# A hybrid decoder layer: side lanes load a step ahead, low-half stores one weight later, lane transposes tied to main products

## The chip, the core and the metric

The kernel runs on one core of a Trainium2 chip. The metric is the time of one execution on the device in microseconds (us). The kernel before was run three times: 2049.04, 2053.64 and 2055.61 us, median 2053.64 us. One of its executions was also taken by the hardware profiler; views of it are called the profile or the trace here.

## The reference

The layer works on 2048 tokens of width 1024 in float32. Cut to what is computed:

```python
hn = rms_norm(h, mix_pre_g)
proj = hn @ w_in                      # 1024 -> 512 q, 128 k, 128 v, 2 x 512 conv
attn_out = sliding_window_attention(q, k, v, attn_sinks, rel_bias)   # window 128, 8 heads
conv_out = conformer_conv(u, ...)     # GLU, causal depthwise conv of 31 taps,
                                      # LayerNorm over channels, silu, 512 x 512
mixed = jnp.concatenate([attn_out, conv_out], axis=-1) @ w_out
h = h + rms_norm(mixed, mix_post_g)
hn = rms_norm(h, ffn_pre_g)
ff = (jax.nn.silu(hn @ w_gate) * (hn @ w_up)) @ w_down               # inner width 2816
h = h + rms_norm(ff, ffn_post_g)
```

## The kernel before

Every matrix product keeps float32 accuracy by splitting each operand into a high and a low half and adding three matmuls: high by high, high by low, low by high (`three`, L170; `product`, L846). So a weight that is loaded (tile `raw`, two buffers) is turned into a tile `w` (six buffers) of two halves: ScalarE copies the high half (L110), GpSimd or VectorE subtracts it for the low half (L112 or the helper of L85). The first time that a weight of w_in or w_out is used, the low half is also stored to DRAM (`lo_in`, `lo_out`, L114, issued from SyncE, whose queue is called SP here); later uses load it (L109) instead of subtracting again. `weight` (L120) issues the load of `raw` and calls `split_w` for its two parts.

Tokens are taken in four tiles of 512. The labels behind the @ of a tile's name tell the stage:

- A0 to A3: the product with w_in. B0 to B3: attention. T0 to T3: the 31 taps of the convolution, on VectorE, whose result is stored to `y_scr` (L547).
- C0 to C3 (`stage_tail`): four blocks of `y_scr` are loaded (tile `fc`, three buffers, L559), transposed on TensorE into the one bank `ct` (`turner`, L531), evicted by ScalarE into `yt` (L532), normalised, transposed back (`conv_tail`, L584) and multiplied by the pointwise weights.
- W0 to W3 (`stage_w`): the product with w_out. Its inputs come from `mixT` in DRAM, two of eight blocks at a time (tile `fa` in W0, `at` of two buffers in W1 to W3, L679), and are split into halves by `acts` (L681 and VectorE). Two weights and eight output banks follow for each two blocks; the first banks are evicted into `mid` by ScalarE (L652). The norm at its end uses x@W (L735, GpSimd).
- H0 and H2: the normed rows of two tiles (`hn_scr` in DRAM) become the operands of the feed-forward part, which is computed by seven products of halves of its matrices instead of eight, so that sums of column blocks are needed. `load_cols` (L755) loads one block of 128 columns, `turned` transposes it in four pieces of 128x128 (L777) into a bank `tr`, ScalarE evicts it (L797). `stage_h_plain` makes the operands B11 and B21 and stores them to `hT`; `stage_h_sums` loads them back (`own`, L812) and makes B22 and the sums T1 to T4.
- F (`stage_pre`, `stage_p1`, L846) and G (`stage_p2`, L1116): the products with w_gate and w_up, and with w_down, for tiles 0 and 1, then for tiles 2 and 3.

The order of the work is written as generators. One main generator (`run`) emits A0 to A3, W1, F, G, F, G. Beside it stand lanes (`Lane`): B, the taps, C, W0, W2, W3, H. Each `yield` of the main generator gives its estimated time to every lane as credit, and a lane emits its next step while it has credit; the step's own `yield` takes its cost away again. So the numbers behind `yield` in a lane are its pacing. When all is emitted, a scheduler orders the instructions of each engine by emission order as priority and by when their inputs and buffers are expected to be ready. An ordering dependency without a semaphore (`after_first`, "NoSync") can force one instruction behind another. On the chip, each engine takes its instructions in the built order, and so do the queues that issue DMAs.

The tiles are in rings of few buffers: `raw` 2, `w` 6, `at` 2, `fc` 3, `fa` 4, `chl` 5, `gb` 2; the banks are `mm` 4, `tr` 3, `ct` 1.

Of the kernel before, what the change touches and what calls it, by code (L numbers as in the profile page):

```python
# [12 lines left out]
F32 = mybir.dt.float32  # L13
# [12 lines left out]
P = 128  # L26
# [11 lines left out]
def layer_kernel(ctx, tc, x, xT, cols, rows, sinks, relb, onehot, w_in, w_pw, w_out, w_gate, w_up, w_down, out):  # L38
# [62 lines left out]
    vtt = dve(nc.vector.tensor_tensor)  # L101
    vts = dve(nc.vector.tensor_scalar)
    ptt = nc.gpsimd.tensor_tensor
    mat = nc.tensor.matmul

    def split_w(raw, tag, low=None, made=False, on_pool=True):
        w = tag if not isinstance(tag, str) else hl(tag)
        if made:
            nc.sync.dma_start(w[:, 1].bitcast(F32), low)  # L109
        act(w[:, 0], raw, AF.Copy)  # L110
        if not made:
            (ptt if on_pool else vtt)(w[:, 1], raw, w[:, 0].bitcast(F32), ALU.subtract)  # L112
            if low is not None:
                nc.sync.dma_start(low, w[:, 1].bitcast(F32))  # L114
# [42 lines left out]
    def after_first(first, r):  # L157
        tc.add_manual_dep(
            r.ins,
            first.ins.name,  # L160
            mybir.DependencyInfo(mybir.DependencyClass.NoSync, mybir.DependencyReason.DATA),
            reason="both halves of the array start together",
        )

    def three(o, pairs, first=True, last=True):
# [361 lines left out]
    def turner(yt, ycs):  # L527
        def turn(c):
            b = ct()
            for s in range(4):  # L530
                nc.tensor.transpose(b[:, s * P : (s + 1) * P], ycs[c][:, s * P : (s + 1) * P], ident)  # L531
# [18 lines left out]
    def stage_tail(t):  # L550
        L = f"C{t}"
        lab[0] = L
        yt = t_("yt", (P, 4, 4 * P))
        ycs = []
        turn = turner(yt, ycs)
        for c in range(4):
            lab[0] = L
            y = f2("fc")
            nc.sync.dma_start(y, y_scr[c, :, t * T : (t + 1) * T])  # L559
            ycs.append(y)  # L560
            turn(c)
            yield 0.5
        yield from conv_tail(t, yt)

    def conv_tail(t, yt):
# [15 lines left out]
        for c in range(4):  # L581
            b = ct()
            for s in range(4):
                nc.tensor.transpose(b[:, s * P : (s + 1) * P], yt[:, s, c * P : (c + 1) * P], ident)  # L584
# [85 lines left out]
    def stage_w(w, spill, G, atag, htag, mtag, bank_of, norm=None, ready=None):  # L670
        L = f"W{w}"
        lab[0] = L
        acc = [f4(atag) for _ in range(4)]

        def acts(gi):
            aa = []
            for c in range(G * gi, G * gi + G):
                m = f2(mtag)
                nc.sync.dma_start(m, mixT[c, :, w * T : (w + 1) * T])  # L679
                a = hl(htag)  # L680
                act(a[:, 0], m, AF.Copy)  # L681
                vtt(a[:, 1], m, a[:, 0].bitcast(F32), ALU.subtract)
                aa.append([a])
            return aa

        nxt = acts(0)
        for gi in range(KC // G):
            aa = nxt
            for n in range(2):
                lab[0] = L  # L690
                if n == 1 and gi + 1 < KC // G and not (ready and G * gi + G == 4):
                    nxt = acts(gi + 1)
                ws = weight(w_out[2 * gi : 2 * gi + 2, :, n * T : (n + 1) * T].rearrange("c p t -> p c t"),
                            lo_out[n, 2 * gi : 2 * gi + 2], w > 0)
                yield from block_half(acc, list(zip(aa, ws)), n, gi == 0, L, bank_of)
            if ready and G * gi + G == 4:
                for i, c in enumerate(ready()):
                    if i == Q0 // 2:
                        ld.until("C1")
                        lab[0] = L  # L700
                        nxt = acts(gi + 1)
                    yield c
        tail = norm_w(w, spill, acc, mtag)
        if norm:
            norm(tail)
        else:
            yield from tail
# [62 lines left out]
    }  # L770
    COLTAG = {0: ["fc", "at", "fc", "at"], 2: ["fc", "at", "fc", "at"]}

    def turned(w, k, bank_of, tag):
        c = load_cols(w, k, tag)
        b = bank_of()
        for s in range(4):
            nc.tensor.transpose(b[:, s * P : (s + 1) * P], c[:, s], ident)  # L777
        return b

    def op_tile(ws, ops, n, k, spare):  # L780
# [23 lines left out]
    def stage_h_sums(ws, ops):  # L804
        L = f"H{ws[0]}"
        spare = {}
        for k in range(4):
            lab[0] = L
            ct_ = COLTAG[ws[0]]
# [12 lines left out]
            lab[0] = L  # L822
            stt(r[:, 0], b12, g1, own[0], ALU.mult, ALU.subtract)
# [410 lines left out]
    class Lane:  # L1234
# [12 lines left out]
        def pump(self, dt):  # L1247
# [3 lines left out]
            while self.items and self.credit > 0:  # L1251
# [5 lines left out]
                p0 = tc.cur_priority  # L1257
                tc.cur_priority = p0 + self.lag
                paced[0] = self.lag > 0
                try:  # L1260
                    c = next(gen)
                    self.credit = 0.0 if c is None else self.credit - c
# [2 lines left out]
                    self.items.pop(0)  # L1265
                tc.cur_priority = p0
                paced[0] = False

        def until(self, name):
            while name not in self.done:  # L1270
                assert self.items, name
                n, gen, needs = self.items[0]
                assert not needs or needs(), n
                for c in gen:
                    assert c is not None
                self.done[n] = clk[0]
                self.items.pop(0)

# [182 lines left out]
```

## Time and profile before

| | |
|---|---|
| time, median of three runs | 2053.64 us |
| the profiled execution's own time | 2048.51 us |
| its span | 2046.7 us |
| its mean granted TensorE clock | 0.987 |
| TensorE busy | 1962.1 us, 96% |
| VectorE busy | 1504.6 us, 74% |
| ScalarE busy | 985.5 us, 48% |
| GpSimd busy | 397.9 us, 19% |
| DMA, mean rate | 221 GB/s |

In the profile PE is TensorE's matmuls and transposes, PEld its weight loads, which overlap them, DVE VectorE, ACT ScalarE, POOL GpSimd, and SP the queue of SyncE that issues most of the DMAs. A line such as L777 is a line of the kernel before; L85 is the helper through which every VectorE instruction is recorded, so VectorE's work is told apart by tile names. "x@W<-fa@W,x@W" means that a tile x of a W stage is written from tiles fa and x. In a row of waits, the three numbers are us in all, times, and the longest. The granted clock (PEclk) is the share of TensorE's full clock that its throttle let through.

### The profile page before, as it was taken

What the parts mean: (1) busy time and instruction counts of PE and PEld (TensorE: products, weight loads), DVE (VectorE), ACT (ScalarE), POOL (GpSimd) and SP (SyncE); (2) the same over time, 40 slices, a digit from 0 to 9 for tenths busy, and PEclk for the clock granted to TensorE, in tenths of its full rate; (3) what the DMA queues carried; (4) which work ended last, traced back from release to release, by engine and by line L of the source; (5) the groups of instructions that cost most, each with busy time, mean ns of one, the idle gap of its engine ahead of it and who ended that gap; (6) DMA issues with size and microseconds to landing.
All of it is one profiled execution on the core that took longest, in us unless ns stands there. A gap on an engine that the chain in (4) does not pass through costs nothing. (4 is left out here: it accounts for less than half of the span.)

```text
span 2046.7 us, 27185 instructions
## 1 busy us (share of the span) xinstructions
PE 1962.1 (96%) x8826; PEld 1566.1 (77%) x8826; DVE 1504.6 (74%) x2641; ACT 985.5 (48%) x1938; POOL 397.9 (19%) x442
## 2 busy tenths in 40 slices
PE   8999999999988999999989999989999999999997
PEld 6877766776667778778868778877788888888886
DVE  5999896995885889887649985577666665545558
ACT  5355455456546633333346457456644433345443
POOL 4011223333111300000001012115423323221001
PEclk9999999999999999999999999999999999999999
DMA  8787645678559876884486778688954453266654
GB/s 307 257 297 232 201 135 175 191 241 277 189 156 335 284 236 235 287 273 160 140 262 199 230 256 294 188 284 288 343 185 155 160 164 114 99 233 218 203 188 149
DMA packets 235902, 451.44 MB, mean 221 GB/s; under 512 B 23496, under 2 KB 49264, under 8 KB 235760
## 3 DMA queue, kind: packets, MB, share of 16 engines
q1 hardware_dynamic: 215216, 419.30, 62.5%
q10 hardware_dynamic: 20544, 30.42, 4.0%
q8 instruction: 69, 1.13, 0.2%
q14 instruction: 73, 0.60, 0.1%
HBM read 330.60 MB, written 119.02 MB: 220 GB/s over the span
## 5 line engine op out<-in xcount | busy, mean ns | idle before, releaser
L85 DVE SCALAR_TENSOR_TENSOR fc@C<-glu@C,colt,fc@C 128x512 f32<-128x512 f32 x480 | 370.1, 784 | 3.5
L846 PE MATMUL mm@F<-hl@H,w@F 128*128 128x512 f32 x1056 | 253.3, 390 | 2.5 <-ACT mm@F L886 1.6
L1116 PE MATMUL mm@G<-hl@G,hl@G 128*128 128x512 f32 x924 | 230.7, 399 | 8.1 <-DVE x@G L85 5.2
L846 PEld LDWEIGHTS mm@F<-hl@H,w@F 128*128 128x128 f32 x1056 | 197.6, 188 | 44.8 <-ACT mm@F L886 2.4
L170 PE MATMUL mm@A<-hl@A,w@A 128*128 128x512 f32 x840 | 207.2, 398 | 5.4 <-ACT w@A L110 1.6
L1116 PEld LDWEIGHTS mm@G<-hl@G,hl@G 128*128 128x128 f32 x924 | 175.0, 192 | 47.2 <-ACT hl@G L759 7.3
L1116 PE MATMUL mm@G<-w@G,hl@G 128*128 128x512 f32 x876 | 199.7, 389 | 0.4 <-DVE w@G L85 0.4
L759 ACT ACTIVATE w@F<-chl@F 128x512 fp32r<-128x512 f32 x220 | 134.9, 624 | 134.8 <-PE mm@F L846 125.8
L1116 PEld LDWEIGHTS mm@G<-w@G,hl@G 128*128 128x128 f32 x876 | 164.4, 188 | 34.9 <-DVE w@G L85 0.9
L170 PEld LDWEIGHTS mm@A<-hl@A,w@A 128*128 128x128 f32 x840 | 155.9, 189 | 42.4 <-ACT w@A L110 2.2
L85 DVE TENSOR_TENSOR w@F<-chl@F,w@F 128x512 fp32r<-128x512 f32 x198 | 146.3, 743 | 34.0 <-ACT w@F L759 33.5
L846 PE MATMUL mm@F<-ql@H,w@F 128*128 128x512 f32 x528 | 128.5, 392 | 10.2 <-ACT w@F L759 5.8
L846 PE MATMUL mm@F<-mid@H,w@F 128*128 128x512 f32 x528 | 130.4, 392 | 2.5 <-ACT mm@F L886 1.7
L846 PE MATMUL mm@F<-p@H,w@F 128*128 128x512 f32 x528 | 131.8, 395 | 0.0
L846 PE MATMUL mm@F<-x@H,w@F 128*128 128x512 f32 x528 | 125.8, 391 | 2.3 <-ACT fa@F L908 2.3
L846 PEld LDWEIGHTS mm@F<-ql@H,w@F 128*128 128x128 f32 x528 | 98.7, 188 | 33.5 <-ACT w@F L759 6.7
L846 PEld LDWEIGHTS mm@F<-mid@H,w@F 128*128 128x128 f32 x528 | 98.3, 188 | 25.6 <-ACT mm@F L886 3.8
L846 PEld LDWEIGHTS mm@F<-p@H,w@F 128*128 128x128 f32 x528 | 101.0, 192 | 22.0 <-ACT at@F L1007 0.6
L846 PEld LDWEIGHTS mm@F<-x@H,w@F 128*128 128x128 f32 x528 | 98.7, 188 | 23.6 <-ACT fa@F L908 2.8
L170 PE MATMUL mm@W<-w@W,hl@W 128*128 128x512 f32 x384 | 102.1, 411 | 7.5 <-ACT hl@W L681 7.4
L110 ACT ACTIVATE w@A<-raw@A 128x512 fp32r<-128x512 f32 x110 | 67.7, 627 | 85.3 <-PE mm@A L170 57.6
L170 PE MATMUL tr@W<-w@W,ql@W 128*128 128x512 f32 x384 | 99.4, 398 | 6.2 <-ACT mid@W L652 5.2
(301 smaller groups left out, 3375.8 us busy)
## 6 DMA issues: line engine op xcount, KB each, us to landing
mids<-fa@F SPq DMA_DIRECT2D x154, 256.0 KB, 2.8
raw@A<-w_in SPq DMA_DIRECT2D x55, 512.0 KB, 4.8
w@A<-lo_in SPq DMA_DIRECT2D x84, 256.0 KB, 3.5
fc@G<-mids SPq DMA_DIRECT2D x77, 256.0 KB, 3.5
fa@G<-mids SPq DMA_DIRECT2D x75, 256.0 KB, 4.3
gb@F<-keeps SPq DMA_DIRECT2D x72, 256.0 KB, 4.3
raw@W<-w_out SPq DMA_DIRECT2D x32, 512.0 KB, 5.4
w@W<-lo_out SPq DMA_DIRECT2D x48, 256.0 KB, 4.1
```

The costliest lines, as they stand in the source:

```text
L85: r = op(*args, **kw)
L110: act(w[:, 0], raw, AF.Copy)
L170: mat(o, a, b, start=first and i == 0, stop=last and i == n - 1)
L759: act(w[:, 0], x, AF.Copy)
L846: mat(o, w[:, a, ks], op[k][:, b], start=first and n == 0, stop=n == 11, skip_group_check=not first)
L1116: mat(banks[b], p_, q_, start=start and z == 0, stop=stop and z == 2, skip_group_check=True)
```

## The change

Three things are changed.

1. Ties. `mat` now remembers the last matmul that was not emitted by a lane (`lead_pe`). `tied(r)` puts `r` behind it by an ordering dependency without a semaphore. The first of every four transposes of a lane is tied: in `turner` (L531), `conv_tail` (L584) and `turned` (L777).
2. Stores. The store of a weight's low half (L114) is not emitted with the weight but at the next call of `weight`, ahead of what that call emits, and it is tied to the last main matmul emitted by then.
3. Loads. `stage_tail` loads block c+1 of `y_scr` before it transposes block c; `stage_h_plain` loads two column blocks ahead, `stage_h_sums` one step ahead (`own` and two column blocks); `stage_w` splits `acts` into `loads` and `acts`. In W0, loads and conversion stay at the second weight of a pair; in W1 to W3 the loads go to the first weight, the conversions stay at the second. In W1's middle, where eight pieces of F are put in, the loads stay at piece 4 and the conversions go to piece 6. Pacing changes with it: C's blocks cost 1.5 instead of 0.5 and begin with 2.0, and the H stages begin with 3.0.

```diff
-    mat = nc.tensor.matmul
+    inlane = [False]
+    lead_pe = [None]
+
+    def mat(*args, **kw):
+        r = nc.tensor.matmul(*args, **kw)
+        if not inlane[0]:
+            lead_pe[0] = r
+        return r
+
+    def tied(r):
+        if lead_pe[0] is not None and lead_pe[0] is not r:
+            after_first(lead_pe[0], r)
+        return r
+
+    later = []
+
+    def defer(n, emit):
+        later.append([n, emit])
+
+    def run_later():
+        for item in later:
+            item[0] -= 1
+        while later and later[0][0] <= 0:
+            later.pop(0)[1]()
...
             if low is not None:
-                nc.sync.dma_start(low, w[:, 1].bitcast(F32))
+                defer(1, lambda: tied(nc.sync.dma_start(low, w[:, 1].bitcast(F32))))
         return w
 
     def weight(src, low, made, raw=None, on_pool=True):
+        run_later()
         if raw is None:
...
         def turn(c):
             b = ct()
             for s in range(4):
-                nc.tensor.transpose(b[:, s * P : (s + 1) * P], ycs[c][:, s * P : (s + 1) * P], ident)
+                r = nc.tensor.transpose(b[:, s * P : (s + 1) * P], ycs[c][:, s * P : (s + 1) * P], ident)
+                if s == 0:
+                    tied(r)
...
+        def fetch(c):
+            if c < 4:
+                lab[0] = L
+                ycs.append(f2("fc"))
+                nc.sync.dma_start(ycs[c], y_scr[c, :, t * T : (t + 1) * T])
+
+        fetch(0)
+        yield 2.0
         for c in range(4):
-            lab[0] = L
-            y = f2("fc")
-            nc.sync.dma_start(y, y_scr[c, :, t * T : (t + 1) * T])
-            ycs.append(y)
+            fetch(c + 1)
+            lab[0] = L
             turn(c)
-            yield 0.5
+            yield 1.5
...
-        nxt = acts(0)
+        nxt = acts(loads(0))
         for gi in range(KC // G):
             aa = nxt
+            own = gi + 1 < KC // G and not (ready and G * gi + G == 4)
             for n in range(2):
                 lab[0] = L
-                if n == 1 and gi + 1 < KC // G and not (ready and G * gi + G == 4):
-                    nxt = acts(gi + 1)
+                if n == (w == 0) and own:
+                    ms = loads(gi + 1)
+                if n == 1 and own:
+                    nxt = acts(ms)
...
                     if i == Q0 // 2:
                         ld.until("C1")
-                        lab[0] = L
-                        nxt = acts(gi + 1)
+                        ms = loads(gi + 1)
+                    if i == Q0 - 2:
+                        nxt = acts(ms)
                     yield c
...
+        cols = {}
+
+        def fetch(k):
+            if k < 4:
+                lab[0] = L
+                cols[k] = load_cols(ws[0], k + off, COLTAG[ws[0]][k] if ws[0] else "fa")
+
+        fetch(0)
+        fetch(1)
+        yield 3.0
         for k in range(4):
             lab[0] = L
-            b = turned(ws[0], k + off, tr, COLTAG[ws[0]][k] if ws[0] else "fa")
+            b = turned(cols.pop(k), tr)
+            fetch(k + 2)
...
+        def fetch(k):
+            if k < 4:
+                lab[0] = L
+                own = t_("chl", (P, 2, T))
+                nc.sync.dma_start(own, hT[ws[0] // 2][k :: 4].rearrange("j p t -> p j t"))
+                got[k] = own, load_cols(ws[1], k, COLTAG[ws[0]][0]), load_cols(ws[1], k + 4, COLTAG[ws[0]][1])
+
+        fetch(0)
+        yield 3.0
         for k in range(4):
...
-            own = t_("chl", (P, 2, T))
-            nc.sync.dma_start(own, hT[ws[0] // 2][k :: 4].rearrange("j p t -> p j t"))
+            own, c12, c22 = got.pop(k)
             own = own[:, 0], own[:, 1]
-            b12 = turned(ws[1], k, tr, ct_[2])
-            b22 = turned(ws[1], k + 4, tr, ct_[3])
+            b12 = turned(c12, tr)
+            b22 = turned(c22, tr)
...
             act(b[:, 0], b22, AF.Copy, scale=g2)
+            fetch(k + 1)
             yield 1.5
...
                 paced[0] = self.lag > 0
+                inlane[0] = True
                 try:
                     c = next(gen)
...
                 paced[0] = False
+                inlane[0] = False
```

More of the change, by code (lines that the diff above doesn't have):

```diff
@@ L161, in after_first @@
             mybir.DependencyInfo(mybir.DependencyClass.NoSync, mybir.DependencyReason.DATA),
-            reason="both halves of the array start together",
+            reason="order",
         )
@@ L583, in conv_tail @@
             for s in range(4):
-                nc.tensor.transpose(b[:, s * P : (s + 1) * P], yt[:, s, c * P : (c + 1) * P], ident)
+                r = nc.tensor.transpose(b[:, s * P : (s + 1) * P], yt[:, s, c * P : (c + 1) * P], ident)
+                if s == 0:
+                    tied(r)
             th = f2("fc")
@@ L673, in stage_w, with loads, acts @@
         acc = [f4(atag) for _ in range(4)]
-        def acts(gi):
+        def loads(gi):
+            lab[0] = L
+            ms = []
+            for c in range(G * gi, G * gi + G):
+                ms.append(f2(mtag))
+                nc.sync.dma_start(ms[-1], mixT[c, :, w * T : (w + 1) * T])
+            return ms
+        def acts(ms):
+            lab[0] = L
             aa = []
-            for c in range(G * gi, G * gi + G):
-                m = f2(mtag)
-                nc.sync.dma_start(m, mixT[c, :, w * T : (w + 1) * T])
+            for m in ms:
                 a = hl(htag)
@@ L771, in layer_kernel, with turned @@
     COLTAG = {0: ["fc", "at", "fc", "at"], 2: ["fc", "at", "fc", "at"]}
-    def turned(w, k, bank_of, tag):
-        c = load_cols(w, k, tag)
+    def turned(c, bank_of):
         b = bank_of()
         for s in range(4):
-            nc.tensor.transpose(b[:, s * P : (s + 1) * P], c[:, s], ident)
+            r = nc.tensor.transpose(b[:, s * P : (s + 1) * P], c[:, s], ident)
+            if s == 0:
+                tied(r)
         return b
@@ L806, in stage_h_sums @@
         spare = {}
+        got = {}
+        def fetch(k):
+            if k < 4:
+                lab[0] = L
+                own = t_("chl", (P, 2, T))
[3 more added lines that the diff above has]
+        yield 3.0
         for k in range(4):
             lab[0] = L
[L809 removed]
             g1, g2 = g_ffn[:, k : k + 1], g_ffn[:, k + 4 : k + 5]
[L811 to L812 removed]
+            own, c12, c22 = got.pop(k)
             own = own[:, 0], own[:, 1]
[L814 to L815 removed]
+            b12 = turned(c12, tr)
+            b22 = turned(c22, tr)
             r = t_("chl", (P, 2, T))
@@ L1273, in until @@
                 assert not needs or needs(), n
+                inlane[0] = True
                 for c in gen:
                     assert c is not None
+                inlane[0] = False
                 self.done[n] = clk[0]
```

## The prediction

> **What bounds the kernel now.** I read first the busy times and the slices of the page.
>
> ```profile
> span 2046.7 us, 27185 instructions
> PE 1962.1 (96%) x8826; PEld 1566.1 (77%) x8826; DVE 1504.6 (74%) x2641; ACT 985.5 (48%) x1938; POOL 397.9 (19%) x442
> PE   8999999999988999999989999989999999999997
> ```
>
> TensorE is busy for 96% of the span. Adding up every idle stretch between its records gives 73.5 us, all of it before 1500 us, so the last quarter has nothing to win. An undisturbed stretch (1700 to 1720) holds 90 main products of 128x512 in 20.00 us: 0.222 us each, the price of one matmul below. The change removes no instruction; it can only win from idle time and from what follows it. So I read next TensorE's waits (line that waits, what it waits for: us in all, times, longest).
>
> ```profile
> PE tr@B L494 <- POOL p@B L476: 9.6, 5, 4.5
> PE mm@W L170 <- ACT hl@W L681: 7.4, 3, 4.0
> PE mm@F L846 <- ACT w@F L759: 5.8, 2, 3.2
> PE mm@G L1116 <- DVE x@G L85: 5.2, 1, 5.2
> PE tr@W L170 <- ACT mid@W L652: 5.2, 1, 5.2
> PE ct@C L531 <- DMA fc@C<-y_scr: 3.2, 1, 3.2
> ```
>
> These are single stalls, not a steady loss. The windows around the 5.2 us wait in W2 (PE busy, PEld, DVE, ACT, POOL, then granted clock, DMA share, GB/s) show what a stall costs besides itself:
>
> ```profile
> 1045.00:1050.00 5.00, 5.00 (x25) 3.81 (x23) 3.40 (x6) 1.52 (x3) 0.00 (x0) 1.00 0.83 243
> 1051.00:1056.00 5.00, 0.00 (x0) 0.00 (x0) 1.06 (x2) 1.03 (x3) 0.00 (x0) 0.83 0.99 334
> 1056.00:1061.00 5.00, 4.87 (x12) 3.80 (x13) 1.61 (x3) 4.67 (x11) 0.00 (x0) 0.50 0.71 197
> ```
>
> After the gap the clock is 0.50 and 12 matmuls are done in 5 us instead of 25: 2.6 us more are lost. Every gap above about 2.3 us is followed by 3.4 or 6.8 us at 0.50, 47.8 us in all, so some 24 us of work. A lane's short stall is worth up to twice its length.
>
> Then the timeline, for who ends the gaps in the lines that the change touches:
>
> ```profile
> 1054.97 0.63 ACT L681 ACTIVATE ql@W<-at@W 128x512 fp32r<-128x512 f32 x1 [4.74 <-DMA at@W<-mixT]
> 1055.50 1.55 ACT L652 ACTIVATE mid@W<-tr@W 128x512 f32<-128x512 f32 x3
> ```
> ```profile
> 457.67 4.20 POOL L476 TENSOR_SCALAR_AFFINE_SELECT p@B<-p@B 128x512 f32<-128x512 f32 x4
> ```
>
> In W2 ScalarE waits 4.74 us for a block of mixT with three evictions of W2's own banks queued behind that conversion; TensorE waits for those banks. At 457 us GpSimd masks four probability tiles for block B2, late because x@W of W0's norm, which waits for VectorE, stands ahead of them; L494 waits 4.50 us.
>
> **The change, part by part.** The order in which the built instructions stand on each engine holds the same instructions before and after; relative to the longest common order 869 of TensorE's, 683 of VectorE's, 350 of ScalarE's, 39 of GpSimd's and 265 of SP's move. The ties are orderings on the same engine, or on issue only: no operation and no semaphore is added, and I cost them at nothing by themselves. They cost through what moves. I take every stall of before that a touched line ends and look how the built order stands there.
>
> a) H0's first eight column blocks (500 to 530 us). Before, their transposes stand within 72 TensorE instructions, with waits of 0.94, 1.10, 0.93 and 0.86 = 3.8 us. After, they are spread over 156, between W1's products, with loads two blocks ahead. Bounds 0 to 3.8; I take 3.
> b) H0's sums (654 to 676): 0.63+0.28+0.23+0.91+1.00 = 3.05 us, partly for at@H from hn_scr. The first pair stands where it stood; the later three stand 24, 36 and 60 matmuls (5.3 to 13 us) later, with their loads at the same places of SP. Hn_scr's loads land in 2.6, 5.3 and 7.8 us (least, median, most). Bounds 0 to 3.05; I take 2.
> c) C3's last block: 3.17 us for y_scr, then 6.8 us at half clock, 3.4 lost. After, it stands 10 matmuls later (2.2 us): 1 us of wait stays. Bounds 0 to 6.6; I take 2.3 of the wait and 1.5 of the clock, 3.8.
> d) W2 at 1051: at@W has two buffers, and its loads keep their places on SP (689, 693, 694, 700 against 690, 693, 694, 700), so the load is not earlier, whatever the diff says. But two of the three evictions stand ahead of the late conversion now, which hands TensorE 12 more matmuls (2.7 us). Bounds 0 to 5.2+2.6 = 7.8; I take 2.7 and nothing for the clock.
> e) B2 at 457: the masks now stand ahead of x@W on GpSimd, and TensorE has 36 instead of 17 matmuls (4 us) between the transposes that need them and their consumers. Bounds 0 to 4.5 plus 2.6 of clock = 7.1; I take 5.
> f) H2 (1385 to 1470): waits of 1.40, 0.84, 0.50, 0.49, 0.55 and 0.64 = 4.4 us, moved as in a and b. Bounds 0 to 4.4; I take 2.
> g) W1's second half (590): 2.53 us. Its at@W loads still stand on SP behind C1's store of y_scr, which waits for the taps on VectorE until 585 us. Bounds 0 to 5 with the clock; I take 0.
> h) Deferred stores. SP's own waits:
>
> ```profile
> SPq L114 <- POOL w@W L112: 40.4, 11, 8.9
> SPq L114 <- DVE w@A L85: 27.6, 16, 4.8
> SPq L755 <- PE tr@H L777: 10.3, 4, 4.4
> ```
>
> 68 us of SP stand still at L114, in A0 and W0, with the next weights behind them. After the change the raw load stands ahead, but raw has two buffers, and that load itself now waits for the same subtraction to release one. The hold moves, it does not go. A0's gaps behind it are 1.40 and 0.63 us; W0's at 334 is 3.96 with its clock. Bounds 0 to 6; I take 0.5.
>
> Sum: 3+2+3.8+2.7+5+2+0+0.5 = 19 us. Against it stand new stalls: one in ten of TensorE's instructions moves, and lists of such moves make some. The nearest row for the price of one is the 5.2 us at L1116, where a late VectorE result stops everything; I take one, 5 us. Bounds: none, or three of them, 15. Two more places could turn. S2's last transposed block stands 36 instructions later, 64 instead of 100 (14.2 us) ahead of the first product that uses T1; in the trace the last transposes to T1's last low half take 8.6 us (1468.8 to 1477.5), so 5.6 us of cover are left and I cost it at nothing; gone, it would cost the difference. C3's tail starts later by its 2.0 of pacing, in G, where W3 follows; the lane ends long before what needs it.
>
> Net: 14 us. The profiled execution took 2048.51 us, 2046.7 of it span, and 5.1 less than the median of 2053.64; it would be 2034.5, and the median 2039.6. A measurement of this kernel can tell 0.3%, 6.2 us, from no change: faster is below 2047.5, slower above 2059.8.
>
> **Rivals.** *The column loads block SP (slower).* A load a step ahead waits on the in-order SP queue until an earlier transpose has released its buffer (fc three, at two), and that transpose is tied to a main product now. The weights of the main products stand behind it. For it speaks the row L755 above (2.6 us a time, four of 32 column loads) and that weights come just in time:
>
> ```profile
> ACT w@F L759 <- DMA raw@F<-w_gate: 12.9, 6, 3.4
> ```
>
> If all 16 loads of the two sums stages wait 2.6 us, that is 41 us of SP; with half of it reaching TensorE, 21 us, and a to c and f (10.8) lost: 19−10.8−5−21 = −18, or 2071; with a to f kept, 14−21 = −7, or 2061. The likelier is 2061, since d and e lie elsewhere and the transposes' own gain is independent. It decides once a hold exceeds what one raw tile feeds, two products of 12 matmuls or 5.3 us; the longest so far is 4.4. Against it: b's loads keep their places on SP.
>
> *The buffers bind (no change).* As in d and h, a load cannot go ahead of its buffer, so the issue moves and the landing does not; the shifts in order win and lose equally. With half the sum, 9.5, against one and a half new stalls, 7.5, the median is 2051.6, within 0.3%.
>
> *The stalls go, and the clock stays full (faster still).* A shortened stall may cost no clock at all: with a to f at their upper bounds 3.8+3.05+6.6+7.8+7.1+4.4 = 32.75, less 5, it is 27.7, or 2026. Against it, here a gap as short as 2.53 us (590) was followed by half clock, and d leaves about 2.5.
> The Trainium skill ("TensorE: Matmul & The Clock Gate", section "HAM oscillation — how this bites in real kernels") has it that the clock falls only for idle gaps longer than about 3.4 us. By that rule d's rest and c's rest would be free of clock loss, and the sum would be 4.5 us more (2.6 and 1.9). The half clock after 2.53 and 3.17 us of idling disagrees, so I don't count on it.
>
> **How the numbers follow.** Forecast, 2030 to 2047 with 2039.6 the likeliest: 0.50, since each of a to f was seen in the built order and only their sizes are open. All stalls gone, 2026: 0.10. No change, 2051.6: 0.18. Slower, about 2061 and up to 2071: 0.22, which is more than its rows bear alone, because one instruction in ten moves and a new wait can come up at places that had none. Faster 0.60, same 0.18, slower 0.22. For 8 in 10 the range runs from 2026 to 2060: left out are half of the slower case and some of the fastest.
>
> **What would show it.** Right: the waits L494 on L476 fall below 6 us, L531 on y_scr to about 1, those of L777 by half; 1051 to 1061 holds about 12 matmuls more; fewer stretches at clock 0.50 (47.8 us now, about 35). For h, SP's waits of L114 shrink and those of L120 grow by as much. Wrong: L755's waits on tr@H above 20 us with L759 or L110 waiting longer for raw weights (the slower rival), or the same idle sum of 70 us in other places (no change); or a gap of over 5 us where before had none.

## The result, and the profile after

The changed kernel takes 2067.46 us (median of 6 runs, 2063.55 to 2072.49) against 2052.61 us for the kernel before in the same sitting (6 runs, 2046.69 to 2056.76). The ratio is 1.008, with a 95% interval of 1.0066 to 1.0094: slower by 15 us, where 14 us faster was forecast. Ratios leave disturbed executions out (one of late_c_loads, below, took 6880 us).

The page of the changed kernel, its span and its busy times:

```profile
span 2069.5 us, 27154 instructions
PE 1973.7 (95%) x8826; PEld 1569.3 (76%) x8826; DVE 1508.8 (73%) x2641; ACT 987.3 (48%) x1938; POOL 396.4 (19%) x442
```

The work is the same. The waits of TensorE in the changed kernel (line that waits, what for: us in all, times, longest) show what was exchanged. Line numbers have moved: every main matmul is recorded at L108 now, the masks are L500, the column loads L800, the seeding of F's banks L953.

```profile
PE mm@F L108 <- ACT mm@F L953: 10.9, 6, 2.6
PE tr@B L108 <- POOL p@B L500: 10.3, 5, 4.5
PE mm@F L108 <- DVE gb@F L85: 8.6, 8, 2.2
PE mm@G L108 <- DVE x@G L85: 5.4, 1, 5.4
PE tr@B L108 <- DVE ql@A L85: 5.3, 1, 5.3
PE mm@F L108 <- ACT fa@F L975: 4.7, 1, 4.7
...
PE tr@W L108 <- ACT ql@W L722: 3.8, 4, 1.8
...
PE tr@W L108 <- ACT mid@W L686: 1.0, 1, 1.0
...
PE tr@H L821 <- DMA at@H<-hn_scr: 0.2, 1, 0.2
```

Three of the rows that the prediction aimed at are nearly gone: 5.2 us of W2's evictions are 1.0, the 3.2 us for y_scr has no row at all, and of 5.8 us of lines tr@H, 0.2 are left. The fourth and largest, the masks' row, did not shrink: 9.6 us before, 10.3 now. The wait of 4.5 us at 457 is gone, but a wait for an earlier attention block's masks, near 290 us, grew from 2.23 to 4.49 (below). In the place of the others stand rows that before had small or not at all: the seeding of F's banks (3.3 us before, 10.9 now), gb@F (2.3, now 8.6), ql@A (5.3) and fa@F (2.7, now 4.7). Idle time between TensorE's records went from 73.5 to 85.1 us, and time at clock 0.50, without the last stretch of the span, from 47.8 to 61.4 us. Neither number is steady from run to run, as the control below shows.

To see where the time went I put the two traces, and that of a control with almost the order of before (w_loads_only, below), side by side at equal TensorE work. Each matmul is given its usual spacing (0.227 us for 512 columns, from start to start; the 0.222 of the prediction counts two of its 90 products that reach over the window's ends), and what the next one starts later than that is counted as lost. The table is worked out from the records of the three traces.

| stretch (us in before) | stage | before | control | changed | changed − control |
|---|---|---|---|---|---|
| 0–95 | A0 | 13.3 | 12.6 | 10.8 | −1.8 |
| 95–183 | A1, B0 | 7.6 | 7.5 | 13.4 | +5.9 |
| 183–274 | A1, A2, B1 | 11.1 | 10.2 | 10.0 | −0.2 |
| 274–469 | A2, A3, W0, C0, C1 | 35.7 | 36.3 | 48.8 | +12.5 |
| 469–565 | W1, H0 | 15.5 | 16.7 | 10.5 | −6.2 |
| 565–666 | W1, B3, F | 21.2 | 26.3 | 26.5 | +0.2 |
| 666–927 | F, H0's sums | 21.2 | 25.5 | 26.5 | +1.0 |
| 927–1097 | G, C2, W2 | 9.9 | 9.4 | 4.3 | −5.1 |
| 1097–1265 | G, C3, W3 | 8.1 | 7.0 | 6.1 | −0.9 |
| 1265–1523 | G, F, H2 | 17.4 | 17.6 | 25.3 | +7.7 |
| all | | 161.0 | 169.1 | 182.2 | +13.1 |

The changed kernel wins 14 us in five stretches and loses 27 in the others. Of the loss, 18 us lie between 95 and 470 us, beside A1 to A3, W0, attention and the first two tails, C0 and C1. C0's and C1's loads and pacing are part of the change, and the prediction's list a to h has no entry for them.

### The profile page after: what moved, and what is told of

The parts are those of the page before. It is cut to its first block, busy times and chain, and to the rows that moved or that the text cites. A ratio compares the mean times of both kernels' runs of the same rounds, so it can differ in the third digit from the quotient of the medians.

```text
span 2069.5 us, 27154 instructions
## 1 busy us (share of the span) xinstructions
PE 1973.7 (95%) x8826; PEld 1569.3 (76%) x8826; DVE 1508.8 (73%) x2641; ACT 987.3 (48%) x1938; POOL 396.4 (19%) x442
## 4 chain that ended last, share of the span: by engine, by line
PE 61%; DMA 16%; DVE 14%; issue 4%; ACT 3%; POOL 2%; SPq 1%; DVEq 0%; ACTq 0%; POOLq 0%
PE mm@F L108 28%; PE mm@G L108 12%; PE mm@A L108 10%; DVE fc@C L85 4%; PE tr@B L108 3%; PE mm@W L108 3%; PE tr@W L108 2%; DMA at@W<-mixT 2%; PE ct@C L108 1%; DVE hl@G L85 1%; DMA td<-wx@G 1%; DMA mixT<-gb@C 1%; DVE w@F L85 1%; DMA wx@G<-w_down 1%; DVE chl@F L85 1%
## 5 line engine op out<-in xcount | busy, mean ns | idle before, releaser
L108 PE MATMUL mm@F<-hl@H,w@F 128*128 128x512 f32 x1056 | 254.2, 390 | 7.3 <-ACT mm@F L953 7.3
L108 PE MATMUL mm@G<-hl@G,hl@G 128*128 128x512 f32 x924 | 229.2, 396 | 10.2 <-DVE x@G L85 5.4
L108 PEld LDWEIGHTS mm@F<-hl@H,w@F 128*128 128x128 f32 x1056 | 197.8, 188 | 49.8 <-ACT mm@F L953 8.6
L108 PEld LDWEIGHTS mm@G<-hl@G,hl@G 128*128 128x128 f32 x924 | 173.6, 190 | 49.8 <-ACT hl@G L804 8.6
L108 PE MATMUL mm@A<-hl@A,w@A 128*128 128x512 f32 x840 | 204.2, 395 | 3.1 <-DVE hl@A L85 1.3
L108 PE MATMUL mm@G<-w@G,hl@G 128*128 128x512 f32 x876 | 199.7, 389 | 0.7 <-DVE w@G L85 0.7
L108 PEld LDWEIGHTS mm@G<-w@G,hl@G 128*128 128x128 f32 x876 | 164.4, 188 | 35.1 <-DVE w@G L85 1.1
L108 PEld LDWEIGHTS mm@A<-hl@A,w@A 128*128 128x128 f32 x840 | 155.2, 188 | 38.8 <-DVE hl@A L85 2.6
L108 PE MATMUL mm@F<-mid@H,w@F 128*128 128x512 f32 x528 | 131.8, 396 | 7.5 <-ACT mm@F L953 3.6
L108 PE MATMUL mm@F<-ql@H,w@F 128*128 128x512 f32 x528 | 128.7, 391 | 5.9 <-DVE p@G L1196 2.6
L108 PE MATMUL mm@F<-x@H,w@F 128*128 128x512 f32 x528 | 128.3, 396 | 6.2 <-ACT fa@F L975 4.7
L108 PE MATMUL mm@F<-p@H,w@F 128*128 128x512 f32 x528 | 129.1, 389 | 0.0
L108 PEld LDWEIGHTS mm@F<-mid@H,w@F 128*128 128x128 f32 x528 | 99.6, 190 | 30.5 <-ACT mm@F L953 4.3
L108 PEld LDWEIGHTS mm@F<-x@H,w@F 128*128 128x128 f32 x528 | 100.2, 191 | 28.1 <-ACT fa@F L975 5.1
L108 PEld LDWEIGHTS mm@F<-ql@H,w@F 128*128 128x128 f32 x528 | 98.7, 188 | 28.1 <-DVE p@G L1196 3.1
L108 PEld LDWEIGHTS mm@F<-p@H,w@F 128*128 128x128 f32 x528 | 99.0, 188 | 20.8 <-ACT at@F L1074 0.4
L108 PE MATMUL mm@W<-w@W,hl@W 128*128 128x512 f32 x384 | 107.1, 418 | 6.6 <-ACT hl@W L722 4.0
L108 PE MATMUL tr@W<-w@W,ql@W 128*128 128x512 f32 x384 | 99.1, 396 | 4.8 <-ACT ql@W L722 3.8
```

The source lines that it names most:

```text
L108: r = nc.tensor.matmul(*args, **kw)
```

## The experiments

**First, the parts alone.** Theory: the loss is new stalls that come from the reshuffled order of the lanes, whichever part shuffles it. Rival: the content of a part costs (loads ahead, SyncE's queue). Each of these kernels is the kernel before with one part of the diff.

Ties of the lane transposes:

```diff
+                r = nc.tensor.transpose(...)
+                if s == 0:
+                    tied(r)
```

> The kernel before with the ties of the lane transposes alone; loads and stores as before. By the theory that the loss is new stalls between 290 and 490 us that come from the reshuffled order of lane B, W0 and the norms (whatever part shuffles them), and that W2's and C3's gaps end by the loads: this moves 605 of TensorE's instructions, so it loses there too, ratio 1.002 to 1.008, and keeps the waits of 5.2 us at 1051 and 3.2 us at 1202. By the rival that the loads taken ahead are what costs, the ties alone are within 0.998 to 1.002.

Measured: 1.006 (1.0044 to 1.0077). The waits at 1051 and 1202 do not stay, against what I expected: W2's is 1.2 us and C3's 0.3, with their loads at the old place.

```profile
PE ct@C L555 <- DMA fc@C<-y_scr: 0.3, 1, 0.3
```

So the ties alone make the two wins, and still lose more elsewhere. The transposes now come later: the last block is stored at 1213.5 us, loaded from 1217.9 and transposed at 1226.5, 8.7 us after the load's issue where before has 3.1. The loss is not between 290 and 490 us (its trace has lost 68.1 us by 469, the control's 66.6) but from 1265 to 1523, beside H2: 29.5 us for the control's 17.6. The size was right and the place wrong.

Deferred stores:

```diff
-                nc.sync.dma_start(low, w[:, 1].bitcast(F32))
+                defer(1, lambda: tied(nc.sync.dma_start(low, w[:, 1].bitcast(F32))))
```

> The kernel before with the deferred and tied stores of low halves alone. It moves 258 of TensorE's instructions. By the theory of the reshuffled order: A0 gains some 3 us (its gaps of 1.40 and 0.63 and the half clock at 34 us go), and 0 to 8 us are lost between 100 and 490 us; ratio 0.998 to 1.004. By the rival that the loads ahead are what costs: 0.998 to 0.999, the gain in A0 alone.

Measured: 1.0047 (1.0028 to 1.0066), just above the range of the first theory and outside the rival's. A0's half clock stays (32.8 us). The wait for y_scr stays at 3.2.

C's early loads and pacing:

```diff
+        fetch(0)
+        yield 2.0
         for c in range(4):
+            fetch(c + 1)
             turn(c)
-            yield 0.5
+            yield 1.5
```

> The kernel before with the early loads and the new pacing of the convolution's tail alone (yield 1.5 for 0.5, 2.0 at its start). By the theory of the reshuffled order: the 3.2 us wait for y_scr at 1202 and its half clock go (6 us), and 5 to 15 us are lost between 290 and 490 us, ratio 0.999 to 1.006. By the rival that loads ahead block the queue of SyncE: more than 10 us of new waits of weights' loads behind the loads of fc@C, ratio over 1.004, with the loss spread over C0 to C3. If neither: 0.997.

Measured: 1.0144 (1.0125 to 1.0164), the dearest part by itself and above the first theory's range. The rival's number fits, its signs do so in part only: ScalarE's waits for raw weights are no longer than before (15.1 us for w_in's, 15.3 before), and the loss lies from 274 to 565 us (20 us more than the control's by then, and still 21 at the end). That is beside C0 and C1, and not spread over C0 to C3. So SyncE's queue is not what costs, but that the content of C0's and C1's part costs is not refuted by this run; the fourth group comes back to it. The wait that these loads are about does not go, it grows:

```profile
PE ct@C L555 <- DMA fc@C<-y_scr: 5.7, 2, 4.1
```

H's early column loads and pacing:

```diff
+        fetch(0)
+        fetch(1)
+        yield 3.0
         for k in range(4):
-            b = turned(ws[0], k + off, tr, ...)
+            b = turned(cols.pop(k), tr)
+            fetch(k + 2)
```

> The kernel before with the early column loads and their pacing in the H stages alone. By the rival of the slower case (SyncE's queue held by column loads that wait for transposes): waits of L755 on tr@H above 20 us, ScalarE waits longer for raw weights, ratio 1.004 or more, with the loss beside H0 and H2. By the theory of the reshuffled order: these waits stay near 10 us or fall, H0's and H2's transposes wait 5 us less, and the loss, if any, is where lane B runs beside W1 (490 to 620 us); ratio 0.997 to 1.004.

Measured: 1.0094 (1.0076 to 1.0112). The time is the rival's, but not its signs: SyncE's waits for tr@H are 16.5 us, not above 20, and with the ties alone, where no load moves, they are 16.2. Nor is the place H0: up to 1445 us the trace has lost 164.7 us for the control's 166.2, and all 20 us more come behind it, in H2's sums, where TensorE waits five times in a row for the seeding of F's banks and then 3.7 us for a weight's conversion.

The four alone lose 12.3, 9.6, 29.5 and 19.3 us by these ratios (of 2051), some 70 together, and the change that holds them all loses 16. Effects that add up badly by so much are not prices that can be added; parts may also mend what others break.

**Second, a control and nudges that hold nothing of the change.** The control takes the W stages' early loads alone:

```diff
+                if n == (w == 0) and own:
+                    ms = loads(gi + 1)
                 if n == 1 and own:
-                    nxt = acts(gi + 1)
+                    nxt = acts(ms)
```

> The kernel before with the early mixT loads of the W stages alone. It moves 14 of TensorE's 8739 instructions and one of VectorE's, so both theories expect 0.999 to 1.001, and W2's wait near 1051 to stay at about 5 us, since at has two buffers. It is the control: a kernel whose order is almost that of before.

Measured: 0.9998 (0.9985 to 1.0011), with W2's wait at 3.5 us. Its page reads

```profile
span 2055.0 us, 27185 instructions
```

8.3 us more than the profile of before at almost the same order and the same median. So single profiles of one kernel differ by that much, and a stretch of the table is to be read only where it differs from the control.

The nudges change one rate of the lanes' pacing in the kernel before:

```diff
-    RC0, RC1, RC2, RC3, RW0, RW, RB, LC = 0.7, 1.1, 0.4, 0.9, 1.7, 1.25, 0.8, 100
+    RC0 = 0.72   (nudge_taps)      RB = 0.82   (nudge_attn)
+    RW  = 1.28   (nudge_wlane)     RB = 0.78   (nudge_attn2)
```

> The kernel before with nothing of the change; only the rate at which the first taps stage is paced goes from 0.70 to 0.72. It moves 591 of TensorE's instructions. By the theory that any reshuffle of the lanes' order costs (the order before was one of the good ones, and what the parts do is not what costs): 1.003 to 1.012, with new single stalls of 2 to 6 us and more time at half clock. By the rival that the parts of the change cost by their content: 0.998 to 1.002.

Measured: 1.0097 (1.0075 to 1.0119).

> The same with the attention lane's rate at 0.82 for 0.80, which moves 384 of TensorE's instructions. Any reshuffle costs: 1.003 to 1.012. The content costs: 0.998 to 1.002.

Measured: 1.0106 (1.0088 to 1.0125).

> The same with the rate of the lane of C2, W2, C3 and W3 at 1.28 for 1.25, which moves 401 of TensorE's instructions, all of them late (beside G, after 1030 us). Any reshuffle costs: 1.001 to 1.005, since less of the kernel is touched and all of it in G and H2. The content costs: 0.998 to 1.002. Up to 1030 us it should run as before, in either case.

Measured: 1.0007 (0.9994 to 1.0019): this reshuffle, which begins after 1030 us, costs nothing that can be told. (Parts of the change that reach only the late stages cost 0.14 to 0.32%, below.)

> Nothing of the change; the attention lane's rate at 0.78 for 0.80. The order stands as before for TensorE's first 2302 instructions (to about 510 us) and 139 move behind them. If any reshuffle costs in proportion to what is moved: 1.001 to 1.003; if a few places decide (H0 and W1's end, 500 to 700 us), up to 1.006; if the stalls between 290 and 490 us are the only dear ones, 0.999 to 1.001.

Measured: 1.0035 (1.0023 to 1.0046), inside the middle range: 139 instructions from 510 us on suffice.

So a rate changed by 2 or 3% in a lane that the change does not touch can cost as much as the whole change: two of the four did, and one cost half as much. Where the time goes in the nudged kernels is the same kind of row as in the changed one. Of nudge_taps:

```profile
PE mm@F L846 <- ACT mm@F L886: 25.9, 15, 3.6
```

and of nudge_attn:

```profile
PE mm@F L846 <- ACT mm@F L886: 15.1, 14, 2.3
```

This row is 3.3 us in before, 4.4 in the control, 10.9 in the changed kernel. It is F's second half, whose banks are first filled from partial sums in DRAM (`keeps`, through the two buffers of gb) by ScalarE. In the changed kernel's trace beside H0's sums these loads stand on SyncE's queue among the column loads, and the fillings on ScalarE behind the lane's conversions (L899). That the row's growth makes the nudged kernels' loss is read from their waits; no run took it away.

**Third, the change by halves.** The late half has the ties and loads in C2, C3 and H2 and the loads of all W stages, but no deferred stores; the early half is the complement.

```diff
+        ea = t >= 2            # C stages;  ws[0] == 2 in H;  the reverse in the early half
+        if ea:
+            fetch(0)
+            yield 2.0
```

> The change in the late stages alone: ties and early loads of C2, C3 and H2, early loads of all W stages, no deferred stores; C0, C1 and H0 as before. TensorE's first 4230 instructions (of 8739) stand as before. By the theory that the change loses by the reshuffled order beside A, W0, W1 and F and wins at W2 and C3: this keeps the wins (6 us at W2, 6 us at C3 in the changed kernel's profile against before) and loses 0 to 6 in H2, ratio 0.995 to 1.000. By the rival that the content of the parts costs wherever it stands: 1.002 or more.

Measured: 1.0032 (1.002 to 1.0045). The win at W2 is there: 3.7 us lost where the control loses 9.5. C3's wait is gone too (0.4 us), but from 1097 to 1265 us 8.9 us are lost for the control's 7.0, and from 1265 to 1523 us 25.2 for 17.6. I had expected no more than equal.

> The complement: ties and early loads of C0, C1 and H0 and the deferred stores; C2, C3 and H2 as before. By the theory of the early reshuffle: all of the loss and none of the wins at W2 and C3, ratio 1.008 to 1.014. If the late stages held the loss: below 1.004.

Measured: 1.0132 (1.0112 to 1.0152). This holds all of the loss and more: +27 us, and its trace has lost 15 us more than the control's by 469 us, as the changed kernel's has (16).

> The early loads and the pacing of C2 and C3 alone, nothing else of the change. If C3's wait for y_scr (3.2 us and 6.8 us at half clock) is cured by the load a step ahead: 0.996 to 0.999, and the wait of L531's line on y_scr below 0.5 us. If its loads are bound by the three fc buffers: the wait stays and the ratio is 0.999 to 1.003.

Measured: 1.0027 (1.0016 to 1.0039), and the wait stays:

```profile
PE ct@C L555 <- DMA fc@C<-y_scr: 4.9, 1, 4.9
```

By the numbers the second reading holds, but the reason for this wait is neither of the two that I named. On SyncE's queue of this kernel:

```profile
1198.87 0.32 SPq L571 DMA_DIRECT2D y_scr<-fc@C  x1
...
1202.85 0.32 SPq L584 DMA_DIRECT2D fc@C<-y_scr  x1
```

The last block of taps is stored at 1198.9 us and loaded back at 1202.9. A load cannot stand a step ahead of data that is only now being written; what helps is to let the transposes come later, and this the ties do. With C2's and C3's loads at 0.27% and all four tails' at 1.44%, most of that part's loss belongs to C0 and C1.

**Fourth, is it content or order?** The same nudges, on the changed kernel. If the change costs by its content, the losses add; if the kernel before has an unusually good order that any early reshuffle leaves, they do not.

> The changed kernel with the first taps stage's rate at 0.72 for 0.70, the nudge that made the kernel before 0.97% slower; 939 of TensorE's instructions move against the changed kernel. If the change costs by its content, the nudge's loss adds to it: 1.014 to 1.020 against before. If the kernel before is a lucky order and the changed one an ordinary one, the nudge moves it to another ordinary one: 1.004 to 1.013.

Measured: 1.0121 (1.0101 to 1.014).

> The changed kernel with the attention lane's rate at 0.82 for 0.80, the nudge that made the kernel before 1.06% slower. Content: 1.015 to 1.021 against before. Lucky order: 1.004 to 1.013.

Measured: 1.0126 (1.0106 to 1.0145).

> The changed kernel with the attention lane's rate at 0.78 for 0.80, the nudge that made the kernel before 0.35% slower; 68 of TensorE's instructions move against the changed kernel. Content: 1.010 to 1.014 against before. Lucky order: 1.005 to 1.011, since so little moves.

Measured: 1.0075 (1.0061 to 1.009).

All three lie in the range of the second reading and below that of the first. Kernel by kernel:

| pacing | without the change | with it | difference |
|---|---|---|---|
| as given | 1 | 1.008 | +0.80% |
| taps 0.72 | 1.0097 | 1.0121 | +0.24% |
| attention 0.82 | 1.0106 | 1.0126 | +0.20% |
| attention 0.78 | 1.0035 | 1.0075 | +0.40% |

The three nudged pairs differ by 0.28% on average, some 6 us; the pair as given by 15. So of the change's 15 us, about 9 would be the order that is left, by this estimate; what remains may be the change's own price or the scatter of three orders. The estimate is weak: each ratio is known to about 0.2 points, and all four differences have the same sign.

Nor is luck the only reading of losses that do not add: a nudge and the change can also delay the same stretch, which is then lost once. Worked out in the way of the table for every trace (within 2 us of it where both have a number), the stretch from 274 to 469 us, where the change lost 12.5, loses 34 to 38 us in twelve of the thirteen kernels without C0's and C1's early loads and pacing, before and control among them; the thirteenth, attention at 0.82, loses 49. All seven kernels that have them lose 47 to 55, through all three nudges. So in this stretch before is an ordinary kernel, and the loss comes with that part of the change. One stall shows how. TensorE in before, then in the changed kernel:

```profile
287.83 1.94 PE L494 MATMUL tr@B<-p@B,vtok 128*64 128x512 f32 x8 [2.23 <-POOL p@B L476]
```
```profile
292.61 3.47 PE L108 MATMUL tr@B<-p@B,vtok 128*64 128x512 f32 x8 [4.49 <-POOL p@B L500]
```

From the last transpose of these probabilities to the products that use them 6.80 us pass in before and 6.77 in the changed kernel. Before has 20 main products to fill them with, the changed kernel 10; ten products of 0.227 us are the 2.26 us by which the wait grew. Near 290 us all seven kernels with the part have 8 to 10 products there and wait 4.27 to 5.38 us, the thirteen others have 18 to 20 and wait 1.90 to 3.08. No run separates its loads from its pacing, and what makes the rest of the 12.5 us was not taken apart.

**Fifth, one stall by its cause.** The longest new stall between 95 and 565 us is at 478 us. VectorE's timeline of the changed kernel (start, us, engine, line, operation, tiles, idle time before and releaser), and then TensorE's:

```profile
471.68 0.16 DVE L85 SCALAR_TENSOR_TENSOR sm@C<-sm@C,sm@C 128x4 f32<-128x4 f32 x1 [5.52 <-POOL sm@C L163]
471.84 8.53 DVE L85 SCALAR_TENSOR_TENSOR x@W<-x@W,sm@W,gb@W 128x512 f32<-128x512 f32 x8
480.29 2.35 DVE L85 TENSOR_TENSOR x@W<-fa@W,x@W 128x512 f32<-128x512 f32 x2
482.56 0.68 DVE L85 SCALAR_TENSOR_TENSOR ql@A<-mm@A,ql@A 128x512 fp32r<-128x512 f32 x1
```
```profile
483.29 0.58 PE L108 MATMUL tr@B<-kz,ql@A 64*128 64x256 f32 x2 [5.28 <-DVE ql@A L85]
```

VectorE idles 5.5 us for the reciprocal square roots of C1 on GpSimd, where the masks of B2 are now mixed in between the steps. Then it runs ten passes of W0's norm in a row, and the 0.7 us drain of ql@A that attention needs stands behind them. From within the stall on, 6.8 us are at half clock (480.1 to 486.9). The test takes those chains off GpSimd:

```diff
-        r = rsqrt(mv[:, :, 1], 4, 1.0)
+        r = rsqrt(mv[:, :, 1], 4, 1.0, t != 1)
-        r = rsqrt(ssq, 4, D, w < 3)
+        r = rsqrt(ssq, 4, D, 0 < w < 3)
```

(The edit reaches the first of W0's two roots, at L763; the second stays on GpSimd.)

> The changed kernel with the reciprocal square roots of C1 and of W0's norms on VectorE instead of GpSimd (VectorE: 18 instructions more, GpSimd: 24 fewer). In the changed kernel's trace VectorE idles 5.5 us for that chain at 466 to 472 us, then runs ten passes of W0's norm, and the drain of ql@A behind them makes TensorE wait 5.3 us, with 6.8 us at half clock behind it. If this queue is the cause of that stall: it goes, 5 to 9 us less, ratio 1.003 to 1.006 against before, and nothing longer than 2 us stands between 460 and 490 us. If the stall only shows work that is late anyway, the same time is waited elsewhere before 520 us: 1.007 to 1.010.

Measured: 1.007 (1.0055 to 1.0084). The stall of 5.28 us is gone, with a shorter one where TensorE goes on:

```profile
477.91 0.66 PE L413 MATMUL mm@A<-ident,fa@A 128*128 128x128 f32 x4 [2.73 <-ACT fa@A L404]
```

The stretch around it, 440 to 500 us in before, loses some 3 us less. So the queue is the cause of that stall, but half of its gain comes back as another wait at once, more than the 2 us that I allowed, and the whole kernel shows 2 us at most (2065.33 against 2067.46), inside its uncertainty. The ratio is the lower end of the second reading's range: for the kernel's time, the stall for the most part only showed work that was late anyway.

**Last, what might beat both.** The late C and W parts without H2, and the freed knot in the kernel before.

> Ties and early loads of C2 and C3 and the early loads of the W stages, without anything in H2 or in the early stages; 445 of TensorE's instructions move against before, all after the first 4230. The late half of the change was 1.0032, with 6 us won at W2 and some 7 us more lost in H2 than in the control. If H2's part is what lost there: 0.996 to 1.000. If the late order as such lost: 1.002 to 1.004.

Measured: 1.0014 (1.0001 to 1.0028). W2's win stays (3.9 us lost for the control's 9.5), but from 1097 to 1265 us, beside C3 and W3, some 5 us more are lost than in the control. From 1265 to 1523 us it loses 21.0 us: 4 fewer than the late half, 3 more than the control, with nothing changed in H2. So about half of that loss is H2's part and half the late order, as far as single traces can tell 4 us.

> The kernel before with nothing of the change, with the reciprocal square roots of C1 and of W0's norms on VectorE instead of GpSimd; 250 of TensorE's instructions move. Its own wait at 457 us (4.5 us for masks behind x@W, then half clock) has GpSimd in the same knot. If the knot is what costs: that wait shrinks below 2 us and the ratio is 0.996 to 0.999. If what is moved costs more than the knot, as with the nudges: 1.001 to 1.008.

Measured: 1.0013 (1.0 to 1.0026), the second reading's range. In its trace the wait for the masks at 458 us is 2.01 us instead of 4.50, and a wait of 2.63 for ql@A follows at 463.6:

```profile
458.06 1.94 PE L494 MATMUL tr@B<-p@B,vtok 128*64 128x512 f32 x8 [2.01 <-POOL p@B L476]
463.64 0.39 PE L426 MATMUL tr@B<-kz,ql@A 64*128 64x256 f32 x2 [2.63 <-DVE ql@A L85]
```

The knot is a few us of work on three engines that all come due at once; untied on one, it tightens on the next. No version here beats the kernel before.

## Why the prediction was wrong

The step that failed is the last term of the sum: "I take one, 5 us" for new stalls, "Bounds: none, or three of them, 15". Against the control the changed kernel lost 27 us in the stretches that grew. I sized this term by one row of the old trace and looked only where before had a stall. C0 and C1, whose loads and pacing the change moves as it does C3's, stand nowhere in the sum, so they were put at nothing without a reason; the stretch beside them lost 12.5 of the 27 us. Even at its upper bound, 15, the term would have been 12 short, and that decided the sign. How much of the other 15 or so is the price of parts and how much the chance of a new order stays open; the nudges show that chance alone can be as large.

The gains look nearly right, 19 us forecast and 14 there, but that is luck. Parts b, c, e and f, 12.8 us of the 19, brought 0.9 us at most in their stretches; the rest comes from W1 with H0 (6.2 for a's 3), W2 (5.1 for d's 2.7) and A0 (1.8 for h's 0.5).

Point by point:

- a, H0's first blocks (3 us): right. From 490 to 560 us TensorE is busy without a gap.
- b, H0's sums (2): the transposes' waits went (0.2 us are left in all of tr@H), but their work crowds the seeding of F's banks. Between 670 and 697 us TensorE waits 1.18, 1.57, 1.98 and 2.59 us for L953, 7.3 us, where before had 1.6. No gain.
- c, C3 (3.8), and d, W2 (2.7): the waits went, W2's with the whole of its half clock. C3's stretch wins only 0.9 us against the control, since W3's product waits there now for a converted input (1.8 us at 1154, then 3.4 at half clock). The windows where W2's gap was (us, PE busy, PEld, DVE, ACT, POOL, clock, DMA share, GB/s):

```profile
1069.00:1074.00 5.00, 4.62 (x24) 3.55 (x23) 3.94 (x6) 2.15 (x5) 0.00 (x0) 1.00 0.90 265
1074.00:1079.00 5.00, 3.97 (x18) 2.92 (x17) 1.39 (x2) 2.54 (x6) 0.00 (x0) 1.00 0.99 350
1079.00:1084.00 5.00, 5.00 (x25) 4.09 (x24) 2.67 (x5) 4.72 (x10) 0.00 (x0) 1.00 0.97 343
```

  18 matmuls stand in the middle window where there were none, and 25 in the next instead of 12. I took the loads out of d rightly, and credited c to loads; the runs show that the ties alone make both.
- e, B2's masks at 457 (5): the move on GpSimd came as the built order showed, and the stall moved one engine on, to VectorE: 5.28 us and the clock. This is the plainest error of reading. It is also the prediction's own sign of being wrong, a gap of over 5 us where before had none. I asked what stood behind the masks on GpSimd, and not who waits for the chain that the masks now delay.
- f, H2 (2): no row of tr@H is left there, but its stretch loses 7.7 us more than the control's.
- g (0): right, no gain. h (0.5): right. Of the 68 us of holds at L114, 16 are left at the store (L137), and some 40 have passed to the raw load (L144):

```profile
SPq L144 <- POOL w@W L135: 20.3, 6, 7.3
SPq L144 <- DVE w@A L85: 19.6, 6, 4.3
...
SPq L137 <- POOL w@W L135: 16.2, 4, 7.1
```

  A0 gained 1.8 us against the control.

The slower rival gave 2061 to 2071 and the measured time lies there, but its mechanism is not what happened. Its two rows in the changed kernel, SyncE's and ScalarE's, both fell, from 10.3 and 12.9 us:

```profile
SPq L800 <- PE tr@H L821: 5.0, 3, 4.3
```
```profile
ACT w@F L804 <- DMA raw@F<-w_gate: 3.5, 4, 1.5
```

What the 0.22 of the slower case also named, that one instruction in ten moves and new waits come up where there were none, is in part what happened. It should have been a rival of its own, with a larger chance and a price of several stalls.

The rival that stalls go with their clock (2026) was held against the half clock after 2.53 us. That example was misread: the half clock that begins at 590.1 us begins 0.2 us into that gap, and 1.6 us after the end of one of 3.14. The 2.58 us gap that ends at 897.5, with half clock from 897.3 on, would have served. The half clock is cheaper to start than I wrote ("every gap above about 2.3 us"), and not as regular: already in before it comes at 33.8 us after a gap of 1.40, and does not come after one of 2.34 at 629.5. In the changed kernel it comes after a gap of 1.14 us:

```profile
101.00:104.60 3.60, 2.46 (x15) 1.27 (x13) 0.71 (x3) 3.00 (x6) 0.00 (x0) 1.00 1.03 400
104.60:108.00 3.40, 3.40 (x8) 2.07 (x8) 3.40 (x8) 1.95 (x4) 0.00 (x0) 0.50 1.05 399
```

That one event, 6.8 us at 0.50 from 104.6 us on or 3.4 us of work, is over half of the 5.9 us lost between 95 and 183. The Trainium skill ("TensorE: Matmul & The Clock Gate", section "HAM oscillation — how this bites in real kernels") gives the rule as no idle gaps of TensorE above about 3.4 us. The trace disagrees here by a factor of three: 2.46 us of 3.60 were busy, and the clock fell.

## What to carry to other kernels

A kernel whose order of instructions is computed by a scheduler, and which beats its neighbours, may stand on a good draw: a change that reshuffles it must first earn back that draw, here 9 us of 15 by a weak estimate. Before pricing the parts of such a change, nudge a rate that has nothing to do with it and see what a reshuffle alone costs; that number is the term for new stalls. Then compare stretch by stretch over all traces: a loss that comes back with one part of the change, whatever the nudge, belongs to that part, as beside C0 and C1 here. And when a built order shows an instruction moved ahead on one engine's queue, ask which chain it now delays there and who, on another engine, has something short queued behind that chain.

## What the runs showed of the hardware that I had not expected

The clock fell to 0.50 after a single idle gap of 1.14 us in a stretch that was 68% busy (2.46 of 3.60 us), and it stays there for 3.4 or 6.8 us at a time, in eight of the twenty traces once for 10.2. A gap of 2.34 us in before did not bring it. So some stalls cost several times their length (1.14 us, and 3.4 us of work at half clock). Profiles of kernels with all but 14 of TensorE's instructions in the same order differ by 8.3 us in span and by 17 us in time at half clock (47.8 and 64.8, without the span's end), while their medians agree within 0.02%: a difference of a few us between two single traces is not yet an effect.
